# Two more slots for split weights, in which small operands lie in pairs, and a planner that knows turns at PSUM banks, 64-row operations and rows of loads

## The chip, the cores and the metric

The kernel runs on one core of one Trainium2 chip. The core has TensorE (PE in the profile, with PEld for its weight loads), VectorE (DVE), ScalarE (ACT), GpSimd (POOL) and SyncE (SP), which issues most of the loads. The metric is the device time of one execution, in microseconds (us); smaller is better.

## The reference

A decoder trunk of two layers, for 256 tokens of width 1024 and 256 memory tokens. Layer 0 mixes tokens by a gated MLP (12 groups of 64, chunks of 128), layer 1 by causal attention (12 heads of 64). Beside either mixer runs a cross-attention of 4 heads into the memory tokens. After each mixer and each feed-forward stands a LayerNorm with a scaled residual.

```python
def swiglu(x, w_in, w_out):
    g, u = jnp.split(x @ w_in, 2, axis=-1)
    return (jax.nn.silu(g) * u) @ w_out

def reference(x, mem, ...):
    for i in range(DEPTH):                       # 2
        if i % 2 == 0:
            h = x @ a_w_in[li]
            u, v, q_mem = jnp.split(h, [W_MIX, 2 * W_MIX], axis=-1)
            mix = gmlp_mixer(u, v, ...)          # gelu(u) * (W_s layer_norm(gelu(v)) + b), W_s causal
        else:
            h = x @ b_w_in[li]
            q, k, v, q_mem = jnp.split(h, ...)
            mix = moba_attention(q, k, v)        # 256 tokens are one block: causal attention
        mem_out = memory_cross_attention(q_mem, mem, w_mem_kv[i])
        sub = jnp.concatenate([mix, mem_out], axis=-1) @ w_mix_out[i]
        x = layer_norm(ALPHA * x + sub, ln_mix_g[i], ln_mix_b[i])
        x = layer_norm(ALPHA * x + swiglu(x, w_ffn_in[i], w_ffn_out[i]), ln_ffn_g[i], ln_ffn_b[i])
    return x
```

All is float32. D_FF is 2816, eleven chunks of 256 columns.

## The kernel before

**Products.** A float32 operand is split into two halves in the fp32r form: `hi`, a cast (ACT), and `lo = x - hi` (DVE). A product is three passes, hi·hi, hi·lo and lo·hi (`PASSES`). In the feed-forward, the first product of most pairs of chunks goes by Strassen and Winograd's seven products `M1` to `M7` in place of eight. They need sums of weight blocks and of x blocks (`Aa`, `Ac`, `SfM`, `SgM`), and their results are put together from PSUM (`Xf`, `Yf`, `Zf` for layer 0, with g for layer 1) into `m1`, `m5` and so on. `sgf` is the silu of a gate, `m5f` the gated chunk before it is transposed (`tpf`), and `htf` the transposed chunk, split in two halves for the second product (`fof`).

**Weights.** Weights come in units of 1 MB (128 x 2048 float32) into six buffers `raw_*`. Each unit is two halves, and each half takes one slot `spl_*` (128 x 2 x 1024): the ACT CAST writes its hi, then the DVE TENSOR_TENSOR its lo. `HALF_BUFS` is the number of these slots. A raw buffer is free for the next load when the lo of its last half is done; some units are then made from others, by a DVE addition in place or by an accumulating load that POOL issues. Loads are issued by SP (hard queue in the code) and POOL (soft queue), in the order of need.

**Small operands.** `ht` (transposed chunks), `memT` (transposed memory tokens) and `qks` (the queries of a pair of heads) are [128, 2, 512] each and have four buffers of their own, tag `hm`.

**Attention.** `stack_k` and `stack_q` move 64-row halves of a projection: `kkm` (hi, ACT casts of 64 rows) and `klm` (lo, DVE on 64 rows) for the memory keys, `qks` and `klq` for layer 1. Scores `s`, exponentials `pb` with row sums `zb`, transposes `pt` to `pT`, then `pv` and the mixed tile `mix1_n`, which is split too: an ACT cast, then a DVE subtraction. The output projection takes `spl_o1_*` halves (`opc`). It is followed by the LayerNorm and by the transposes of its result into `x3T` (x1T in layer 0), and there the feed-forward of the layer begins.

**What sets the order.** No instruction stands in the order of the program's text. `Plan` records all operations, `deadlines()` gives each a due time counted back from TensorE's order, and `simulate()` runs the recorded operations through a cost model (`Op.cost`, and class `Wire` for loads), choosing at each step the operation that can start first and is due first. It does so five times, with other settings (`TRIALS`), and the order with the least idle TensorE is issued by `emit()`. TensorE's own order is that of the text. Operations added by `either` (copies and scalings) may go to ACT or DVE, whichever the plan gives them to. On the chip each engine runs its list strictly in order, each instruction waiting on semaphores for what it reads or overwrites. So every recorded instruction has the line of `emit`, L574, and is told apart by its tiles.

Of the kernel before, what the change touches and what calls it, by code (L numbers as in the profile page):

```python
# [34 lines left out]
RAW_BUFS = 6  # L35
HALF_BUFS = 10
NFF = D_FF // 256
# [150 lines left out]
class Buffer(View):  # L188

    def __init__(self, pool, space, tag, bufs, shape, dtype, name):  # L190
# [9 lines left out]
        self.psum, self.whole = pool == "ps", False  # L200
        self.tile, self.log, self.slot, self.left, self.last = None, [], None, 0, 0.0


class Op:
    def __init__(self, n, engine, name, args, kw):
# [5 lines left out]
        self.before, self.after, self.opens = {}, [], []  # L211
        self.late, self.other = None, None
        self.cost()

# [30 lines left out]
class Wire:  # L245

    HARD, SOFT, BOTH, LANES = ((7000, 250), (30000, 370), (1e12, 428)), 223, (155, 123), 8
    SPARE = 1200, 1800

# [6 lines left out]
    def issue(self, op, t):  # L256
        self.run(t, [self.hard, self.soft])
        if op.engine == "sync":
            self.sent.append(op)
        (self.soft if op.engine == "gpsimd" else self.hard).append([op, t + 2350, op.bytes])  # L260
        self.run(1e12, [[list(x) for x in q] for q in (self.hard, self.soft)])

    def run(self, until, queues):
        hard, soft = queues
        now = self.now
        while (hard or soft) and now < until:
# [5 lines left out]
            for q, r, a in zip(queues, rates, live):  # L272
                if a:
                    q[0][2] -= (stop - now) * r
                    if q[0][2] < 1:
                        op = q.pop(0)[0]
                        op.end = stop + 100
                        op.sure = stop + (self.SPARE[op.engine == "gpsimd"] if stop > 20000 else 200)
            now = stop
# [4 lines left out]
class Plan:  # L284
# [90 lines left out]
    def order(self):  # L375
        self.deadlines()
        best = None
        for trial in self.TRIALS:
            for op in self.ops:
                for b in op.roots:  # L380
                    b.slot, b.last, b.left, b.moves = None, 0.0, 0, []
            for op in self.ops:
# [11 lines left out]
    def simulate(self, slip, idle, margin):  # L394
        lost, table, whole = 0, None, set()
        by_late = {e: sorted((op for op in self.ops if op.engine == e), key=lambda op: (op.late, op.n)) for e in ("vector", "scalar")}
# [27 lines left out]

        def opening(op):

            t0 = max([at[op.n]] + [o.sure for o in op.moves])
            if op.engine == "sync":
# [35 lines left out]
        while len(out) < len(self.ops):  # L464
            best, again = None, False
            for e in self.ENGINES:
# [4 lines left out]
                else:  # L471
                    cands = ready[e]
                c = [(max(free[e], t), op) for op in cands for t in (opening(op),) if t is not None]
                if not c:
# [39 lines left out]
            if e == "scalar" and op.name == "activation" and op.args[2] not in (AF.Identity, table):  # L514
                table = op.args[2]
                t += 1283
            if e == "tensor" and t > free[e] + 1:
                t += 95
# [38 lines left out]
            for b in op.roots:  # L557
                b.left -= 1
                b.last = max(b.last, end + 35)
                if op.name == "dma_start":  # L560
                    b.moves.append(op)
# [106 lines left out]
def build(chip, tc, ins, out):  # L668
    ET = mybir.EngineType
    with (  # L670
# [322 lines left out]
        class Ffn:  # L993
# [10 lines left out]
            def ht_tile(self, c):  # L1004
                if c not in self.hts:
                    self.hts[c] = tile_of("act", [P, 2, 512], F32R, "hm", f"ht{self.nm}{c}", 4).rearrange(
                        "p s (k t) -> p s k t", k=2)
                return self.hts[c]
# [250 lines left out]
        for j in range(4):  # L1259
            t = tile_of("act", [P, 2, 512], F32R, "hm", f"memT{j}", 4)  # L1260
            split(t[:, 0, :], t[:, 1, :], mraws[j])
# [83 lines left out]
        def qk_half(hp, j):  # L1345
# [3 lines left out]
            if j == 0:  # L1349
                st = tile_of("act", [P, 2, 512], F32R, "hm", f"qks{hp}", 4).rearrange("p a (b t) -> p a b t", b=2)  # L1350
                qks[hp] = st, klq[:, hp % 2]
                stack_q(lambda par: st[:, 0, par, :], t)
# [162 lines left out]
```

## Time and profile before

| what | value |
|---|---|
| runs, us | 564.18, 563.02, 563.37; median 563.37 |
| profiled execution, us | 563.18, its span 561.5 |
| granted TensorE clock, mean | 0.997 |
| PE busy | 548.5 us (98%), 3028 matmuls |
| DVE busy | 503.4 us (90%), 673 instructions |
| ACT busy | 370.0 us (66%), 563 instructions |
| POOL busy | 33.7 us (6%) |
| DMA | 132.52 MB, mean 236 GB/s |

The program runs through layer 0's mixer (to about 96 us), its feed-forward (to about 265), layer 1's projections and attention (to about 372), its feed-forward (to about 554), and 7 us after the last matmul. Rows of the timeline and of the groups name what is written and what is read (`out<-in`) without buffer numbers. In square brackets stands how long the engine was idle before the row and what ended the idle time. A row of several like instructions gives their number (x12). The ends of matmuls are modelled, so where two stretches of TensorE are compared, it is by their starts.

### The profile page before, as it was taken

Reading aid. Unit: us, or ns where it says so; the run is one execution under the profiler, and the core shown is the slowest. Engines: PE = TensorE matmul, PEld = TensorE weight load, DVE = VectorE, ACT = ScalarE, POOL = GpSimd, SP = SyncE. Lnnn points to the kernel's source line nnn. Section 1 sums busy time; section 2 is a strip of 40 time slices with the busy share of each in tenths; the row PEclk is TensorE's granted clock in tenths of the full one; section 3 lists DMA queues with packets and bytes.
Section 4 is the critical chain, followed back from the end, with each engine's and each line's share of the span. In section 5 each row is a group of like instructions: output and inputs, shape, how many; then the busy total and the mean of one; then the engine's idle time right before and its main releaser. Section 6 shows DMA issues by size and latency. Waiting matters only on the chain.

```text
span 561.5 us, 8058 instructions
## 1 busy us (share of the span) xinstructions
PE 548.5 (98%) x3028; PEld 473.2 (84%) x3028; DVE 503.4 (90%) x673; ACT 370.0 (66%) x563; POOL 33.7 (6%) x45
## 2 busy tenths in 40 slices
PE   8999999999999999999999999999999999999995
PEld 7999979878887888887899989788778888888884
DVE  5789979999999989989987898679999999999975
ACT  6876745596649486666466988557857495957620
POOL 2011000000000010000000000100000000100001
PEclk9999999999999999999999999999999999999998
DMA  8999753567897969889557253834488989797902
GB/s 288 400 384 350 306 210 116 149 151 274 204 395 183 375 187 336 253 248 355 222 222 295 84 189 138 163 113 151 86 302 210 392 200 392 176 353 212 296 5 76
DMA packets 23496, 132.52 MB, mean 236 GB/s; under 512 B 2592, under 2 KB 6304, under 8 KB 9376
## 3 DMA queue, kind: packets, MB, share of 16 engines
q1 hardware_dynamic: 20000, 109.45, 50.0%
q0 software_dynamic: 3024, 22.02, 21.1%
q10 hardware_dynamic: 432, 0.52, 0.3%
q8 instruction: 24, 0.39, 0.3%
q14 instruction: 16, 0.13, 0.1%
HBM read 120.46 MB, written 1.05 MB: 216 GB/s over the span
## 4 chain that ended last, share of the span: by engine, by line
PE 61%; DVE 18%; DMA 9%; ACT 6%; issue 4%; SPq 0%; DVEq 0%; ACTq 0%; POOLq 0%
PE fog L574 10%; PE Xg L574 7%; DVE spl_s_M L574 6%; DMA raw_s<-in_w 4%; PE opa L574 4%; PE Zg L574 4%; PE qk L574 4%; PE fof L574 3%; PE pu L574 3%; PE bv L574 3%; PE Xf L574 3%; DMA raw_s<-raw_s 3%; DVE raw_s L574 3%; PE opc L574 2%; PE va L574 2%
## 5 line engine op out<-in xcount | busy, mean ns | idle before, releaser
L574 DVE TENSOR_TENSOR spl_s_M<-raw_s,spl_s_M 128x1024 fp32r<-128x1024 f32 x140 | 164.9, 1225 | 3.2 <-ACT spl_s_M L574 3.0
L574 ACT CAST spl_s_M<-raw_s 128x1024 fp32r<-128x1024 f32 x140 | 139.7, 1051 | 37.9 <-DVE raw_s L574 15.3
L574 ACT CAST spl_w<-raw_w 128x1024 fp32r<-128x1024 f32 x44 | 45.7, 1054 | 29.3 <-DMA raw_w<-in_w 26.2
L574 PE MATMUL fof<-spl_w,htf 128*128 128x512 f32 x264 | 63.9, 392 | 0.0
L574 PE MATMUL fog<-spl_w,htg 128*128 128x512 f32 (+1 forms) x282 | 63.9, 378 | 0.0
L574 PEld LDWEIGHTS fog<-spl_w,htg 128*128 128x128 f32 x282 | 50.1, 188 | 9.4
L574 PEld LDWEIGHTS fof<-spl_w,htf 128*128 128x128 f32 x264 | 49.0, 188 | 9.9
L574 DVE TENSOR_TENSOR spl_w<-raw_w,spl_w 128x1024 fp32r<-128x1024 f32 x44 | 53.7, 1225 | 1.5 <-ACT spl_w L574 1.5
L574 DVE TENSOR_TENSOR raw_s<-raw_s,raw_s 128x2048 f32<-128x2048 f32 x19 | 43.5, 2292 | 0.0
L574 PE MATMUL qk<-x2T,spl_qk 128*128 128x256 f32 x288 | 36.4, 284 | 0.8 <-DVE mix L574 0.8
L574 PEld LDWEIGHTS qk<-x2T,spl_qk 128*128 128x128 f32 x288 | 35.2, 191 | 1.0 <-DVE mix L574 1.0
L574 PE MATMUL Xg<-spl_s_M,SgM 128*128 128x512 f32 x120 | 29.2, 391 | 0.7 <-DVE SgM L574 0.7
L574 PE MATMUL Zf<-spl_s_M,SfM 128*128 128x512 f32 x120 | 29.2, 392 | 0.3 <-DVE htf L574 0.3
L574 PE MATMUL Zg<-spl_s_M,SgM 128*128 128x512 f32 x120 | 28.8, 389 | 0.0
L574 PE MATMUL Xf<-spl_s_M,SfM 128*128 128x512 f32 x120 | 28.8, 389 | 0.0
L574 PE MATMUL Xf<-spl_s_M,x1T 128*128 128x512 f32 x120 | 28.3, 390 | 0.0
L574 PE MATMUL Xg<-spl_s_M,x3T 128*128 128x512 f32 x120 | 28.2, 389 | 0.0
L574 PEld LDWEIGHTS Xg<-spl_s_M,SgM 128*128 128x128 f32 x120 | 22.4, 188 | 5.7 <-DVE SgM L574 1.2
L574 PEld LDWEIGHTS Zf<-spl_s_M,SfM 128*128 128x128 f32 x120 | 22.3, 188 | 5.6 <-DVE htf L574 1.0
L574 PEld LDWEIGHTS Xf<-spl_s_M,x1T 128*128 128x128 f32 x120 | 22.5, 188 | 4.8
L574 PEld LDWEIGHTS Xg<-spl_s_M,x3T 128*128 128x128 f32 x120 | 22.5, 188 | 4.7
L574 PEld LDWEIGHTS Zg<-spl_s_M,SgM 128*128 128x128 f32 x120 | 22.5, 188 | 4.7
(246 smaller groups left out, 1005.0 us busy)
## 6 DMA issues: line engine op xcount, KB each, us to landing
raw_s<-in_w SPq DMA_DIRECT2D x40, 1024.0 KB, 7.4
raw_w<-in_w SPq DMA_DIRECT2D x22, 1024.0 KB, 9.1
raw_s<-in_w POOLq DMA_DIRECT2D x11, 1024.0 KB, 9.0
raw_s<-raw_s POOLq DMA_DIRECT2D x10, 1024.0 KB, 7.8
raw_o<-in_w SPq DMA_DIRECT2D x8, 1024.0 KB, 6.8
raw_qk<-in_w SPq DMA_DIRECT2D x6, 1024.0 KB, 5.1
raw_u<-in_w SPq DMA_DIRECT2D x3, 1024.0 KB, 12.0
raw_bv<-in_w SPq DMA_DIRECT2D x4, 768.0 KB, 8.2
```

The source lines that it names most:

```text
L574: getattr(getattr(self.nc, c.engine), c.name)(*map(real, c.args), **{k: real(v) for k, v in c.kw.items()})
```

## The change

- `HALF_BUFS` goes from 10 to 12, and the four buffers of tag `hm` are gone. Their memory is the same: 12 slots of 8 KB a partition, against 10 and four of 4 KB. `ht` of chunks c and c+1 (chunk 0 alone), `memT` 0 and 1, 2 and 3, and `qks` of an even and the next odd pair of heads lie together in one `spl` slot, which is free again when both are done.
- A PSUM buffer remembers when each engine last used it (`used`), and in the plan an operation on another engine waits for that end plus 35 ns (`turn`).
- In the plan an ACT or DVE operation that works on other rows than the one before it on its engine starts only when that one is done, plus 25 ns (`Op.rows`).
- In the plan of loads the margins `SPARE` go from 1200 and 1800 ns to 600 and 800, and a load that comes in a row behind another, or a soft load that shared the wire, is put 2000 ns later (`SKEW`).

```diff
-HALF_BUFS = 10
+HALF_BUFS = 12
...
+        ap = (self.writes or self.reads)[0].ap
+        self.rows = ap.offset // ap.ap[0][0], ap.ap[0][1]
...
-    SPARE = 1200, 1800
+    SPARE, SKEW = (600, 800), 2000
...
+                    if all(live):
+                        soft[0][3] = True
                     if q[0][2] < 1:
-                        op = q.pop(0)[0]
-                        op.end = stop + 100
-                        op.sure = stop + (self.SPARE[op.engine == "gpsimd"] if stop > 20000 else 200)
+                        op, _, _, burst = q.pop(0)
+                        if q:
+                            q[0][3] = q[0][1] <= stop
+                        op.end = stop + 100 + (self.SKEW if burst and stop > 20000 else 0)
+                        op.sure = op.end + (self.SPARE[op.engine == "gpsimd"] if stop > 20000 else 100)
...
+        def turn(op, e):
+
+            return max([0.0] + [t + 35 for b in op.roots if b.psum for e2, t in b.used.items() if e2 != e])
+
+        def opening(op, e):
+
+            t0 = max([at[op.n], turn(op, e)] + [o.sure for o in op.moves])
...
+            if e in by_late:
+                was, done = rows.get(e, (op.rows, 0.0))
+                if was != op.rows:
+                    t = max(t, done + 25)
+                rows[e] = op.rows, t + op.call.lat
...
+                b.used[e] = end
...
-                    self.hts[c] = tile_of("act", [P, 2, 512], F32R, "hm", f"ht{self.nm}{c}", 4).rearrange(
-                        "p s (k t) -> p s k t", k=2)
+                    mates = [c, c + 1] if c else [c]
+                    t = tile_of("spl", [P, 2, 1024], F32R, "spl", f"ht{self.nm}{c}", HALF_BUFS)
+                    for j, m in enumerate(mates):
+                        self.hts[m] = t[:, j, :].rearrange("p (s k t) -> p s k t", s=2, k=2)
...
-            t = tile_of("act", [P, 2, 512], F32R, "hm", f"memT{j}", 4)
+            if j % 2 == 0:
+                both = tile_of("spl", [P, 2, 1024], F32R, "spl", f"memT{j}", HALF_BUFS)
+            t = both[:, j % 2, :].rearrange("p (s n) -> p s n", s=2)
...
-                st = tile_of("act", [P, 2, 512], F32R, "hm", f"qks{hp}", 4).rearrange("p a (b t) -> p a b t", b=2)
-                qks[hp] = st, klq[:, hp % 2]
+                if hp % 2 == 0:
+                    both = tile_of("spl", [P, 2, 1024], F32R, "spl", f"qks{hp}", HALF_BUFS)
+                    for n in range(2):
+                        qks[hp + n] = both[:, n, :].rearrange("p (a b t) -> p a b t", a=2, b=2), klq[:, n]
+                st = qks[hp][0]
```

What the plan makes of it: TensorE's order stays. The rest moves a little everywhere: DVE has 667 operations where it had 675 and ACT 536 where it had 528, since 20 copies and scalings go from DVE to ACT and 12 the other way. Recorded instructions now have line L590. Three places follow.

The first is DVE where layer 0's feed-forward begins (`klm`: the memory keys' lo; `spl_s0_1_M1_*`: lo of the weights of M1; `Aa10`: a block of x; `x1T`: lo of the feed-forward's input). Before:

```order
L574 SCALAR_TENSOR_TENSOR xres_771<-xres_771,rsa1_1129,gb0mix_650 128x512 x2
L574 TENSOR_TENSOR klm_116<-hkm1_1085,kkm10_1161 64x256 x2
L574 TENSOR_TENSOR klm_116<-hkm1_1085,kkm11_1170 64x256 x2
L574 TENSOR_TENSOR spl_s0_1_M1_0_1068<-raw_s0_1_11_882,spl_s0_1_M1_0_1068 128x1024
L574 COPY Aa10_1214<-pta10_1201 128x512
L574 TENSOR_TENSOR x1T_1092<-pta10_1201,x1T_1092 128x4x128
```

The same place of the changed kernel:

```order
L590 SCALAR_TENSOR_TENSOR xres_746<-xres_746,rsa1_1127,gb0mix_650 128x512 x2
L590 TENSOR_TENSOR spl_s0_1_M1_0_1066<-raw_s0_1_11_887,spl_s0_1_M1_0_1066 128x1024
L590 TENSOR_TENSOR spl_s0_1_M1_1_1078<-raw_s0_1_11_887,spl_s0_1_M1_1_1078 128x1024
L590 TENSOR_TENSOR klm_116<-hkm1_1083,kkm10_1159 64x256 x2
L590 TENSOR_TENSOR klm_116<-hkm1_1083,kkm11_1169 64x256 x2
L590 TENSOR_TENSOR x1T_1090<-pta10_1196,x1T_1090 128x4x128
```

Both halves of M1's lo now stand ahead of the four `klm` operations, and the copy `Aa10` has gone to ACT.

The second is ACT at the first pair of chunks of layer 0's feed-forward (`sgf3`: the gate of chunk 3; `spl_w0_3_0`: hi of weights of the second product; `spl_s0_5_*`: hi of the next pair's weights). Before:

```order
L574 CAST spl_w0_3_0_1724<-raw_w0_3_1664 128x1024
L574 CAST spl_s0_5_M2_0_1739<-raw_s0_5_21_1678 128x1024
L574 ACTIVATE sgf3_1747<-Xf3_1508 128x512
L574 CAST spl_s0_5_M5_0_1753<-raw_s0_5_11_1638 128x1024
L574 CAST spl_s0_5_M5_1_1760<-raw_s0_5_11_1638 128x1024
```

And the same place of the changed kernel:

```order
L590 CAST spl_w0_3_0_1730<-raw_w0_3_1661 128x1024
L590 CAST spl_s0_5_M5_0_1742<-raw_s0_5_11_1635 128x1024
L590 ACTIVATE sgf3_1749<-Xf3_1504 128x512
L590 CAST spl_s0_5_M5_1_1753<-raw_s0_5_11_1635 128x1024
L590 CAST spl_s0_5_M2_0_1762<-raw_s0_5_21_1681 128x1024
```

The cast that reads `raw_s0_5_21`, the unit loaded last, now stands two rows behind `sgf3` and no longer ahead of it; a cast of an older unit has its place.

The third is DVE where layer 1's feed-forward begins (`x3T`: lo of its input; `Ac`: blocks of x; `spl_r1_0_B_1`: lo of the weights of chunk 0; `m1g1`: a product of chunk 1). Before:

```order
L574 TENSOR_TENSOR m1g1_3831<-m1g1_3831,Yg1_3839 128x512
L574 TENSOR_TENSOR spl_r1_0_B_1_3774<-raw_r1_0_B_3341,spl_r1_0_B_1_3774 128x1024
L574 COPY Ac10_3888<-ptc10_3874 128x512
L574 TENSOR_TENSOR x3T_3785<-ptc10_3874,x3T_3785 128x4x128
L574 TENSOR_TENSOR x3T_3785<-ptc11_3879,x3T_3785 128x4x128
L574 TENSOR_TENSOR spl_s1_1_M5_0_3804<-raw_s1_1_11_2941,spl_s1_1_M5_0_3804 128x1024
L574 TENSOR_TENSOR spl_s1_1_M5_1_3812<-raw_s1_1_11_2941,spl_s1_1_M5_1_3812 128x1024
```

And in the changed kernel:

```order
L590 TENSOR_TENSOR m1g1_3823<-m1g1_3823,Yg1_3833 128x512
L590 TENSOR_TENSOR spl_s1_1_M5_0_3829<-raw_s1_1_11_3049,spl_s1_1_M5_0_3829 128x1024
L590 COPY Ac10_3882<-ptc10_3870 128x512
L590 COPY Ac11_3887<-ptc11_3875 128x512
L590 TENSOR_TENSOR x3T_3775<-ptc10_3870,x3T_3775 128x4x128
L590 TENSOR_TENSOR x3T_3775<-ptc11_3875,x3T_3775 128x4x128
L590 TENSOR_TENSOR spl_s1_1_M5_1_3838<-raw_s1_1_11_3049,spl_s1_1_M5_1_3838 128x1024
```

The lo of `spl_r1_0_B_1` has gone up, ahead of the statistics of the second token tile's LayerNorm, and that of `spl_s1_1_M3_0` stands among them, `M5_0` has come ahead of the x3T operations, and the copy `Ac11` has come over from ACT.

More of the change, by code (lines that the diff above doesn't have):

```diff
@@ L200, in __init__ @@
         self.psum, self.whole = pool == "ps", False
-        self.tile, self.log, self.slot, self.left, self.last = None, [], None, 0, 0.0
+        self.tile, self.log, self.slot, self.left, self.last, self.used = None, [], None, 0, 0.0, {}
 class Op:
@@ L259, in issue @@
             self.sent.append(op)
-        (self.soft if op.engine == "gpsimd" else self.hard).append([op, t + 2350, op.bytes])
+        (self.soft if op.engine == "gpsimd" else self.hard).append([op, t + 2350, op.bytes, False])
         self.run(1e12, [[list(x) for x in q] for q in (self.hard, self.soft)])
@@ L380, in order @@
                 for b in op.roots:
-                    b.slot, b.last, b.left, b.moves = None, 0.0, 0, []
+                    b.slot, b.last, b.left, b.moves, b.used = None, 0.0, 0, [], {}
             for op in self.ops:
@@ L394, in simulate @@
     def simulate(self, slip, idle, margin):
-        lost, table, whole = 0, None, set()
+        lost, table, whole, rows = 0, None, set(), {}
         by_late = {e: sorted((op for op in self.ops if op.engine == e), key=lambda op: (op.late, op.n)) for e in ("vector", "scalar")}
@@ L423, in free_at @@
             return max([b.last] + [o.sure for o in b.moves]) if b else 0.0
-        def opening(op):
-            t0 = max([at[op.n]] + [o.sure for o in op.moves])
+        def turn(op, e):
+            return max([0.0] + [t + 35 for b in op.roots if b.psum for e2, t in b.used.items() if e2 != e])
+        def opening(op, e):
+            t0 = max([at[op.n], turn(op, e)] + [o.sure for o in op.moves])
             if op.engine == "sync":
@@ L472, in simulate @@
                     cands = ready[e]
-                c = [(max(free[e], t), op) for op in cands for t in (opening(op),) if t is not None]
+                c = [(max(free[e], t), op) for op in cands for t in (opening(op, e),) if t is not None]
                 if not c:
```

## The prediction, made before the changed kernel was run

> **What bounds the kernel now.** I read the busy times first, then windows of the stages, then TensorE's waits, and then the timelines of three engines at each wait.
>
> ```profile
> PE 548.5 (98%) x3028; PEld 473.2 (84%) x3028; DVE 503.4 (90%) x673; ACT 370.0 (66%) x563; POOL 33.7 (6%) x45
> ```
>
> ```profile
> 116.00:200.00 84.00, 83.49 (x374) 68.38 (x375) 82.02 (x80) 58.67 (x71) 4.92 (x6) 1.00 0.85 275
> 391.00:419.00 28.00, 26.28 (x116) 20.64 (x115) 28.00 (x32) 19.18 (x25) 1.52 (x2) 1.00 0.62 208
> ```
>
> The first fence is from the page: TensorE is busy for 548.5 of 561.5 us. The second gives, by window, the length, then the busy time of PE, PEld, DVE, ACT and POOL, the granted clock, the DMA share and GB/s. DVE works 82.02 of 84 us in one stretch of the first feed-forward, and all 28 us of the start of the second. So TensorE is the bound, and DVE comes close behind it: where DVE is late, TensorE waits. TensorE's order doesn't change and it does the same matmuls, so the change can win only the waits (engine, tile, what it waited for; total, times, longest):
>
> ```profile
> PE qk L574 <- DVE mix L574: 0.8, 1, 0.8
> PE Xg L574 <- DVE SgM L574: 0.7, 1, 0.7
> PE tpf L574 <- DVE hf L574: 0.7, 1, 0.7
> PE tpf L574 <- DVE m5f L574: 0.5, 2, 0.3
> PE tpg L574 <- DVE m1g L574: 0.5, 1, 0.5
> PE tpg L574 <- DVE m5g L574: 0.3, 1, 0.3
> PE tpg L574 <- DVE hg L574: 0.3, 1, 0.3
> PE Zf L574 <- DVE htf L574: 0.3, 1, 0.3
> ```
>
> A shown wait is less than what it costs, because the shown ends of matmuls are modelled. I measure the loss from start to start, with the pace of this row, 2.72 / 12 = 0.227 us for a matmul of 512 columns:
>
> ```profile
> 122.50 2.72 PE Xf L574 x12
> ```
>
> **The change, place by place.** *A, layer 0's feed-forward begins.* TensorE, then DVE (two of four like rows), then ACT (two of three):
>
> ```profile
> 112.53 2.88 PE L574 MATMUL Xf<-spl_s_M,x1T 128*128 128x512 f32 x12
> 116.13 0.88 PE L574 MATMUL tpf<-ident,hf 128*128 128x128 f32 x4 [0.71 <-DVE hf L574]
> ...
> 97.08 0.42 DVE L574 TENSOR_TENSOR klm<-hkm,kkm 64x256 fp32r<-64x256 f32 x1 [0.54 <-ACT kkm L574]
> ...
> 99.65 0.43 DVE L574 TENSOR_TENSOR klm<-hkm,kkm 64x256 fp32r<-64x256 f32 x1 [0.43 <-ACT kkm L574]
> ...
> 97.53 0.37 ACT L574 CAST kkm<-hkm 64x256 fp32r<-64x256 f32 x1 [0.48 <-DVE klm L574]
> ...
> 99.25 0.37 ACT L574 CAST kkm<-hkm 64x256 fp32r<-64x256 f32 x1 [0.48 <-DVE klm L574]
> ```
>
> From 112.53 to 116.13 are 3.60 us for 12 matmuls worth 2.72: 0.88 lost (0.17 more than the shown 0.71; I add 0.16 to the other shown waits). DVE and ACT take turns at `klm` and `kkm`: DVE is idle four times, 0.54 + 3 x 0.43 = 1.83 us. Between there and 116 DVE is full. In the changed order both lo of M1 (1.2 us each) stand ahead of the four `klm`, so ACT's casts have over 2 us to get done, and the copy `Aa10` (a 128x512 DVE operation, 0.69 in place B) goes to ACT. DVE's lead is about 1.83 + 0.6 = 2.4 us, and `hf` wants 0.88. Between 0 (the four still take turns) and 0.88 I take 0.85.
>
> By the Trainium skill (PSUM — Partial Sum Buffer, section on bank collisions), two engines may be at one bank at once if they are in different quadrants of partitions; a cast of the other 64 rows would then not have to wait for `klm`, and the turns would be no fixed cost. By that rule three of the four gaps, some 1.3 us, would have another cause and stay; the lead would be 1.1, and I would set the sum 0.3 lower. The rows here show the casts waiting 0.48 for DVE each time, and the row decides.
>
> *B, the gate of chunk 3, and the wait behind it.* TensorE, ACT, DVE:
>
> ```profile
> 169.70 0.27 PE L574 MATMUL tpf<-ident,m1f 128*128 128x128 f32 x1
> 170.10 0.33 PE L574 MATMUL tpf<-ident,m5f 128*128 128x128 f32 x1
> ...
> 170.84 3.01 PE L574 MATMUL fof<-spl_w,htf 128*128 128x512 f32 x12
> 174.10 1.66 PE L574 MATMUL Zf<-spl_s_M,SfM 128*128 128x512 f32 x6 [0.26 <-DVE htf L574]
> ...
> 165.29 1.06 ACT L574 CAST spl_w<-raw_w 128x1024 fp32r<-128x1024 f32 x1 [4.39 <-DMA raw_w<-in_w]
> 167.78 1.05 ACT L574 CAST spl_s_M<-raw_s 128x1024 fp32r<-128x1024 f32 x1 [1.43 <-DMA raw_s<-in_w]
> 168.73 0.59 ACT L574 ACTIVATE sgf<-Xf 128x512 f32<-128x512 f32 x1
> ...
> 169.35 0.69 DVE L574 SCALAR_TENSOR_TENSOR m5f<-m5f,sgf 128x512 f32<-128x512 f32 x1 [0.94 <-ACT sgf L574]
> 169.96 3.49 DVE L574 TENSOR_TENSOR spl_s_M<-raw_s,spl_s_M 128x1024 fp32r<-128x1024 f32 x3
> 173.37 0.69 DVE L574 TENSOR_TENSOR htf<-tpf,htf 128x512 fp32r<-128x512 f32 x1
> ```
>
> ACT stands at the cast of M2, whose load lands at 167.7, and the gate `sgf` behind it starts at 168.73. In the changed order a cast of a unit that is long there has this place, so `sgf` starts when TensorE's product is done, over 1 us sooner; and `htf`, which has three lo ahead of it here (3.49 us), has one lo and one copy (1.22 + 0.6). The loss is 0.29 at `m5f` (0.40 us between the two transposes; the seven from 170.10 to 170.84 take 0.74, so 0.11 would do) and 3.26 - 2.72 = 0.54 at `Zf`: 0.83. I take 0.7, between 0.3 (the gate alone) and 0.83.
>
> *C, the two shown waits of `m5f`* (0.5 together, with the ends 0.8), at later pairs: the first has the same cause, a gate behind four casts of a unit just landed, and three of these move behind it: 0.4 of 0.43. At the other nothing moves near the gate: 0.1 of 0.37. In all 0.5, between 0 and 0.8.
>
> *D, attention.* TensorE waits for `mix1_0`:
>
> ```profile
> 333.48 2.77 PE L574 MATMUL qk<-x2T,spl_qk 128*128 128x256 f32 x21 [0.76 <-DVE mix L574]
> ...
> 331.87 1.22 DVE L574 TENSOR_TENSOR spl_o<-raw_o,spl_o 128x1024 fp32r<-128x1024 f32 x1
> 333.00 0.42 DVE L574 TENSOR_TENSOR mix<-pv,mix 128x256 fp32r<-128x256 f32 x1
> ```
>
> The loss is 0.76 + 0.15. In the changed order `mix1_0` stands ahead of the scalings of `pb`, and the weight's lo (1.22) is gone from ahead of it: I take 0.7, between 0.3 and 0.91. Against it stands what now gets thin here: the same stage turns more 64-row work round, and the cover of the other scores is small.
>
> ```profile
> 324.33 0.88 DVE L574 TENSOR_TENSOR klq<-qk,qks 64x256 fp32r<-64x256 f32 x2 [0.32 <-ACT qks L574]
> ...
> 325.32 0.28 PE L574 MATMUL s<-klq,qks 128*128 128x128 f32 x1
> ```
>
> `klq` ends at 325.21 for a matmul at 325.32: 0.11 of cover. One lo put ahead of such a step costs up to 1.2. I put 0.7 for new waits, between 0 and 2.4 (two of them in full).
>
> *E, layer 1's feed-forward begins.* TensorE, then DVE:
>
> ```profile
> 400.22 0.71 PE L574 MATMUL Xg<-spl_s_M,SgM 128*128 128x512 f32 x2
> 401.66 1.65 PE L574 MATMUL Xg<-spl_s_M,SgM 128*128 128x512 f32 x6 [0.72 <-DVE SgM L574]
> ...
> 367.44 1.22 DVE L574 TENSOR_TENSOR spl_r_A<-raw_r_A,spl_r_A 128x1024 fp32r<-128x1024 f32 x1 [1.84 <-ACT spl_r_A L574]
> 389.44 0.69 DVE L574 TENSOR_TENSOR x3T<-ptc,x3T 128x512 fp32r<-128x512 f32 x1 [0.65 <-ACT x3T L574]
> 390.42 0.69 DVE L574 TENSOR_TENSOR x3T<-ptc,x3T 128x512 fp32r<-128x512 f32 x1 [0.29 <-ACT Ac L574]
> ```
>
> The losses: `SgM` 1.44 - 2 x 0.227 = 0.99; `hg`, `m1g`, `m5g` (0.3 + 0.5 + 0.3 shown) with the ends 1.5; together 2.5. From 391 to 419 DVE has no gap, so whatever it has done before 391 comes off these waits one for one. Two lo (`r1_0_B_1` and `M3_0`, 1.22 each) go up to where DVE is idle (1.84 in one row); `M5_0` fills the gaps of 0.65 and 0.29; against that the copy `Ac11` comes to DVE (0.6). The lead is 1.2 + 0.9 - 0.6 = 1.5 us until the place of `M3_0`, and 2.7 after it. For the moved lo ACT must cast sooner too, and it needs slots for it; the two more slots give them. The first two waits (1.4) go, and most of the others: I take 1.9, between 0.8 and 2.5.
>
> Edits that cost nothing: pairs in one slot have the same casts and lo as before, of the same sizes; the copies that go to ACT fall on an engine busy 66%; of the loads a few small rows swap places. The tail after 554 keeps its order.
>
> **The sum:** 0.85 + 0.7 + 0.5 + 0.7 + 1.9 - 0.7 = 3.95 us. The profiled execution took 563.18 (span 561.5), so 559.2 in its terms; the median of the runs is 563.37, 0.19 above it, so I predict 559.4. If every loss above went and no new wait came (0.88 + 0.83 + 0.8 + 0.91 + 2.5 = 5.9), it would be 557.5; with the lower ends (0 + 0.3 + 0 + 0.3 + 0.8 - 2.4 = -1.0), 564.4. Some tenths more lie in waits not costed here, so 557.0 is the lower end.
>
> **Rivals.** *The waits only move: no change.* DVE is the bound in all but name (28.00 of 28, 82.02 of 84), its summed work falls by under 2 us of 503, and an order that is early at one place is late at the next. For it: those windows. Against it: in places A and E DVE's gaps before the full stretch are themselves filled (1.83 and 0.94 us), which no later place takes back, since TensorE, not DVE, sets the pace from 419 on. It would give 562.9 to 563.9.
>
> *Half the leads carry.* The gaps at `klm` stay because the casts are in the same turns, and E gains only `SgM`: 0 + 0.7 + 0.3 + 0.4 + 1.0 - 0.7 = 1.7, so 561.7.
>
> *Slower: short slots in the attention make loads late.* `qks` now takes weight slots, and the lo of the `spl_o1` halves stand 8 to 13 us later in DVE's order; a raw buffer is free only after them, so the loads of `raw_r1_0_B` and `raw_s1_1_12`, and POOL's loads behind them, go out later.
>
> ```profile
> 356.56 0.88 POOL L574 DMA_DIRECT2D raw_s<-in_w  x1 [2.61 <-DVE mix L574]
> ...
> DMA to landing us min/median/max: 4.8/7.8/12.6
> ```
>
> The last of them goes out at 356.56 and takes up to 12.6, so lands at 369. I put it 6 us later, at 375, and its cast at about 379 in the changed order: 4 us are to spare. From there each us is one of TensorE's: a load 9 us later than I put it costs 5 us, eats all gains and gives 564.4. Against it: the median load here takes 7.8.
>
> *Planned too close.* The margins of loads fall to half, which would put casts of late units ahead of gates, as in B. The orders I compared show the reverse (the new 2 us push such casts back), so this is part of the half gain.
>
> **How the numbers follow.** What the measurement can tell from no change is about 0.2%, 1.1 us. My forecast (a gain of 2.5 us or more): 0.60. Half the gain (1.1 to 2.5): 0.18. No change: 0.13. Slower: 0.09. Faster is thus 0.78. The range goes from 557.0 to 563.2: it leaves out the slower case, half of no change, and a little at the low end, in all some 0.18. The forecast's own range is 557.0 to 560.9.
>
> **What would show it.** In the profile after, TensorE's waits for `hf`, `htf`, the first `m5f`, `mix` and `SgM` are gone or under 0.2; the four `klm` stand together with no gaps; `sgf` of chunk 3 starts about 1 us earlier against TensorE; DVE between 391 and 419 has gaps again. TensorE's busy time stays at 548. I am wrong if a new wait of over 0.5 stands in the attention (`s` or `qk` waiting for `klq`), if casts wait for DMA right ahead of a gate, or if the load that POOL issues lands after 379.

## The result, and the profile after

The changed kernel takes 557.62 us in the median of four runs (556.42 to 558.08), against 563.64 for the kernel before (563.02 to 564.18): a ratio of 0.989, with a 95% interval of 0.987 to 0.991, so 6.0 us less. Executions more than 1.5% above the fastest of their kernel are left out of all medians and ratios here. The profiled execution took 556.42, with a span of 554.7.

The page's busy times, TensorE's waits (all that are shown), and two windows of the changed kernel; the second window is the stretch that was 391 to 419 before:

```profile
PE 545.8 (98%) x3028; PEld 473.4 (85%) x3028; DVE 502.1 (91%) x665; ACT 371.0 (67%) x571; POOL 34.3 (6%) x45
```

```profile
PE warmup L744 <- DVE mhalf L741: 1.1, 1, 1.1
PE tpf L590 <- DVE m5f L590: 0.7, 2, 0.4
```

```profile
116.00:200.00 84.00, 84.00 (x385) 69.75 (x384) 81.28 (x78) 55.54 (x66) 4.34 (x5) 1.00 0.85 273
...
385.00:412.00 27.00, 27.00 (x122) 21.77 (x121) 26.77 (x31) 17.10 (x24) 1.59 (x2) 1.00 0.60 195
```

Of the eight rows of waits in the prediction one is left, `m5f`. DVE still does 81.28 of 84 us and 26.77 of 27, but TensorE now works all of both windows. TensorE's busy time is 545.8, where I had put 548: with the same 3028 matmuls, 2.7 us of what went had counted as busy. In place A (ACT, DVE, TensorE):

```profile
94.28 3.02 ACT L590 CAST kkm<-hkm 64x256 fp32r<-64x256 f32 x8 [2.78 <-PE hkm L590]
...
95.32 2.35 DVE L590 TENSOR_TENSOR spl_s_M<-raw_s,spl_s_M 128x1024 fp32r<-128x1024 f32 x2
97.59 1.72 DVE L590 TENSOR_TENSOR klm<-hkm,kkm 64x256 fp32r<-64x256 f32 x4
...
114.28 0.60 PE L590 MATMUL tpf<-ident,hf 128*128 128x128 f32 x4
```

The eight casts run in a row, the four `klm` too, without a gap, and `hf` is there in time. In B (ACT, DVE, TensorE) and in D (DVE, TensorE):

```profile
165.74 0.59 ACT L590 ACTIVATE sgf<-Xf 128x512 f32<-128x512 f32 x1
...
166.36 0.69 DVE L590 SCALAR_TENSOR_TENSOR m5f<-m5f,sgf 128x512 f32<-128x512 f32 x1 [0.53 <-ACT sgf L590]
...
168.16 2.98 PE L590 MATMUL fof<-spl_w,htf 128*128 128x512 f32 x12
170.98 1.75 PE L590 MATMUL Zf<-spl_s_M,SfM 128*128 128x512 f32 x7
...
328.01 0.41 DVE L590 TENSOR_TENSOR mix<-pv,mix 128x256 fp32r<-128x256 f32 x1
...
329.65 0.28 PE L590 MATMUL sm<-klm,qqm 128*128 128x256 f32 x1
329.77 1.48 PE L590 MATMUL qk<-x2T,spl_qk 128*128 128x256 f32 x11
```

`Zf` starts 2.82 us after `fof` (3.26 before), and `qk` 0.12 after the last `sm` (0.76 of shown wait before). In E, DVE:

```profile
374.62 1.22 DVE L590 TENSOR_TENSOR spl_r_B<-raw_r_B,spl_r_B 128x1024 fp32r<-128x1024 f32 x1
...
382.25 1.22 DVE L590 TENSOR_TENSOR spl_s_M<-raw_s,spl_s_M 128x1024 fp32r<-128x1024 f32 x1
383.38 1.28 DVE L590 COPY Ac<-ptc 128x512 f32<-128x512 f32 x2
384.73 1.29 DVE L590 TENSOR_TENSOR x3T<-ptc,x3T 128x512 fp32r<-128x512 f32 x2
```

The lo of `r1_0_B_1` and `M5_0` stand where they were to stand, and the gaps of 0.65 and 0.29 ahead of `x3T` are gone.

TensorE's order is the same in every kernel here, so time can be put down to stretches between the same two matmuls. The table gives, for the profile of each run, how much longer a stretch is than in the kernel before, in us, from the starts of the matmuls that bound it. Start: to the 61st matmul. A: to the `Zf` that stands at 142.93 before. B: to 175.83. C: to 265.93. Attention: to 362.62. E: to 419.49. End: the rest. Behind them stand the median of the timed runs and the ratio to the kernel before on the same chip.

| kernel | start | A | B | C | attention | E | end | all but start | median, ratio |
|---|---|---|---|---|---|---|---|---|---|
| before, length | 10.75 | 131.13 | 32.90 | 90.10 | 96.69 | 56.87 | 134.70 | | 563.64 |
| changed | -0.95 | -1.35 | -0.96 | +0.48 | -1.93 | -2.35 | +0.29 | -5.82 | 557.62, 0.989 |
| changed, again | -0.22 | -1.36 | -0.95 | +0.80 | -1.93 | -2.30 | +0.34 | -5.41 | 557.29, 0.9877 |
| slots only | +0.14 | -0.01 | +0.27 | +0.69 | +2.24 | -2.20 | +0.28 | +1.27 | 564.74, 1.0021 |
| slots and load rule | +1.14 | +0.73 | -0.46 | +0.48 | +2.26 | -2.20 | +0.41 | +1.20 | 563.77, 1.001 |
| planner only | +0.19 | -1.37 | -0.95 | -0.97 | -1.90 | +0.11 | -0.09 | -5.17 | 558.39, 0.9912 |
| without load rule | -0.73 | -1.37 | -0.40 | +0.71 | -1.92 | -2.29 | +0.22 | -5.05 | 557.84, 0.9901 |
| without turns | +0.26 | -0.75 | -0.64 | +0.95 | +0.20 | -1.65 | +0.34 | -1.55 | 562.18, 0.9977 |
| without 64-row rule | -0.14 | -1.37 | -0.95 | +0.93 | +0.21 | -2.29 | +0.49 | -3.00 | 560.17, 0.9933 |
| eleven slots | +0.80 | -1.37 | -0.95 | -0.97 | -1.90 | -1.68 | -0.06 | -6.93 | 556.55, 0.9866 |
| m5 moved | -0.57 | -1.36 | -0.95 | -0.39 | -1.90 | -2.35 | -0.06 | -7.01 | 557.41, 0.9883 |
| m5 moved, again | -0.63 | -1.36 | -0.96 | -0.16 | -1.90 | -2.34 | +0.17 | -6.55 | 556.79, 0.9869 |
| before, lo ahead of klm | +0.49 | -0.48 | +0.12 | +0.78 | 0.00 | 0.00 | +0.02 | +0.44 | 563.2, 0.9987 |
| before, casts first | 0.00 | -0.13 | -0.07 | +0.65 | 0.00 | 0.00 | -0.03 | +0.42 | 563.91, 1.0 |

Two things in it are chance. The start has the same order in all kernels, and its length differs by up to 2.1 us from run to run, since TensorE waits there for the first weights (0.3 to 1.6 us in the rows of waits, or none). The 0.73 that "slots and load rule" has in A is of that kind too: the five matmuls behind the 61st lose all of it. And in C the last two kernels have the order of the kernel before, yet lose 0.65 and 0.78 us against its profile: C as a whole is known to some 0.8 us only. Otherwise A, B, attention and E repeat to about 0.1.

### The profile page after: what moved, and what is told of

Same layout as the page of the kernel before. It is cut to its first block, busy times and chain, and to the rows that moved or that the text cites. A ratio compares the mean times of both kernels' runs of the same rounds, so it can differ in the third digit from the quotient of the medians.

```text
span 554.7 us, 7993 instructions
## 1 busy us (share of the span) xinstructions
PE 545.8 (98%) x3028; PEld 473.4 (85%) x3028; DVE 502.1 (91%) x665; ACT 371.0 (67%) x571; POOL 34.3 (6%) x45
## 4 chain that ended last, share of the span: by engine, by line
PE 72%; DVE 14%; DMA 7%; issue 4%; ACT 2%; SPq 0%; DVEq 0%; ACTq 0%; POOLq 0%
PE fog L590 11%; PE Xg L590 10%; DVE spl_s_M L590 7%; PE qk L590 6%; PE Zg L590 5%; DMA raw_s<-in_w 4%; PE opc L590 4%; PE opa L590 4%; PE pu L590 3%; PE bv L590 3%; PE pvm L590 3%; PE Yg L590 2%; PE va L590 2%; PE hkm L590 2%; PE hqm L590 2%
## 5 line engine op out<-in xcount | busy, mean ns | idle before, releaser
L590 DVE TENSOR_TENSOR spl_s_M<-raw_s,spl_s_M 128x1024 fp32r<-128x1024 f32 x140 | 164.7, 1221 | 6.3 <-ACT spl_s_M L590 6.1
L590 ACT CAST spl_s_M<-raw_s 128x1024 fp32r<-128x1024 f32 x140 | 139.6, 1050 | 38.1 <-DMA raw_s<-in_w 23.4
L590 PE MATMUL fof<-spl_w,htf 128*128 128x512 f32 x264 | 63.9, 392 | 0.0
L590 PE MATMUL fog<-spl_w,htg 128*128 128x512 f32 (+1 forms) x282 | 63.9, 378 | 0.0
L590 ACT CAST spl_w<-raw_w 128x1024 fp32r<-128x1024 f32 x44 | 45.6, 1051 | 23.4 <-DMA raw_w<-in_w 20.9
L590 PEld LDWEIGHTS fog<-spl_w,htg 128*128 128x128 f32 x282 | 50.2, 188 | 9.4
L590 PEld LDWEIGHTS fof<-spl_w,htf 128*128 128x128 f32 x264 | 49.0, 188 | 9.9
L590 DVE TENSOR_TENSOR spl_w<-raw_w,spl_w 128x1024 fp32r<-128x1024 f32 x44 | 53.7, 1221 | 2.9 <-ACT spl_w L590 2.9
L590 DVE TENSOR_TENSOR raw_s<-raw_s,raw_s 128x2048 f32<-128x2048 f32 x19 | 43.5, 2288 | 0.1
L590 PE MATMUL qk<-x2T,spl_qk 128*128 128x256 f32 x288 | 36.3, 283 | 0.0
L590 PEld LDWEIGHTS qk<-x2T,spl_qk 128*128 128x128 f32 x288 | 35.2, 192 | 0.0
L590 PE MATMUL Zg<-spl_s_M,SgM 128*128 128x512 f32 x120 | 29.1, 390 | 0.0
L590 PE MATMUL Xg<-spl_s_M,SgM 128*128 128x512 f32 x120 | 29.0, 390 | 0.0
L590 PE MATMUL Zf<-spl_s_M,SfM 128*128 128x512 f32 x120 | 29.0, 390 | 0.0
L590 PE MATMUL Xf<-spl_s_M,SfM 128*128 128x512 f32 x120 | 28.8, 389 | 0.0
L590 PE MATMUL Xf<-spl_s_M,x1T 128*128 128x512 f32 x120 | 28.3, 390 | 0.0
L590 PE MATMUL Xg<-spl_s_M,x3T 128*128 128x512 f32 x120 | 28.3, 390 | 0.1
L590 PEld LDWEIGHTS Xf<-spl_s_M,x1T 128*128 128x128 f32 x120 | 22.4, 188 | 5.2 <-issue 0.6
L590 PEld LDWEIGHTS Xg<-spl_s_M,x3T 128*128 128x128 f32 x120 | 22.5, 188 | 5.1 <-issue 0.4
L590 PEld LDWEIGHTS Zg<-spl_s_M,SgM 128*128 128x128 f32 x120 | 22.5, 188 | 5.0 <-DVE SgM L590 0.4
L590 PEld LDWEIGHTS Xf<-spl_s_M,SfM 128*128 128x128 f32 x120 | 22.5, 188 | 4.7
L590 PEld LDWEIGHTS Xg<-spl_s_M,SgM 128*128 128x128 f32 x120 | 22.4, 188 | 4.8 <-DVE SgM L590 0.2
```

The lines of the kernel that those rows point to most:

```text
L590: getattr(getattr(self.nc, c.engine), c.name)(*map(real, c.args), **{k: real(v) for k, v in c.kw.items()})
```

## The experiments

**One: slots alone.** The changed kernel with the planner of before.

```diff
-    SPARE, SKEW = (600, 800), 2000
+    SPARE, SKEW = (1200, 1800), 0
...
-                        op.sure = op.end + (self.SPARE[op.engine == "gpsimd"] if stop > 20000 else 100)
+                        op.sure = stop + (self.SPARE[op.engine == "gpsimd"] if stop > 20000 else 200)
...
-            return max([0.0] + [t + 35 for b in op.roots if b.psum for e2, t in b.used.items() if e2 != e])
+            return 0.0
...
-                if was != op.rows:
+                if False:
```

> Twelve slots and pairs, with the planner of before (no turns, no 64-row rule, old load margins). By its order klm and kkm still take turns, the cast of M2 still stands ahead of sgf3; mix1_0 stands behind one lo and one scaling; r1_0_B_1 and M5_0 stand ahead of the second LayerNorm of layer 1. Theory (each place follows its own order rows): waits for hf (0.9 us) and for htf and m5f at chunk 3 (0.8) stay, mix falls from 0.9 to under 0.4, layer 1's feed-forward start loses 0.5 to 1.2 in place of 2.5; together about 561.5 us. Rival (the memory is what counts: slots let ACT cast early everywhere): near the changed kernel, 558 us, with hf and htf gone too. Rival (waits only move): 563 us.

Measured: 564.74 us, ratio 1.0021 (1.0008 to 1.0034): slower than before by 0.2%. TensorE's longest waits of this kernel:

```profile
PE tpf L590 <- DVE m5f L590: 1.5, 3, 0.8
PE pt L590 <- DVE mix L590: 1.4, 2, 1.0
PE qk L590 <- DVE mix L590: 1.2, 1, 1.2
PE warmup L744 <- DVE mhalf L741: 1.1, 1, 1.1
PE va L590 <- ACT spl_v L590: 0.9, 1, 0.9
PE tpf L590 <- DVE hf L590: 0.7, 1, 0.7
```

The theory held for A and B, gave E too little (2.20 for 1.3 to 2.0, nearly all that E gets in the end), and failed for the attention: `mix` was to fall under 0.4 and rose to 1.2, with 1.4 more at the transposes behind it. The gain of E is lost again there.

**Two: slots and the load rule.** As before, but with `SPARE, SKEW = (600, 800), 2000`.

> Slots and pairs and the plan's later loads (SPARE, SKEW), without turns and without the 64-row rule. By its order the gates of chunks 3 and 7 stand ahead of the casts of late units, klm and kkm still take turns. Theory: waits at chunk 3 (0.8) are gone, hf (0.9) stays, the rest as with slots alone: about 560.7 us. Rival (the load rule puts casts too late and PE waits for weights): over 562 us with PE waiting for spl tiles.

Measured: 563.77 us, 1.001 (1.0 to 1.0021), with the waits of the attention as in the first run. Against slots only, the load rule makes B 0.73 shorter, for 0.8 expected, and nothing else that can be told from chance. The wait for `htf` is gone, but `m5f` at chunk 3 still waits 0.22 us, though its gate stands ahead of the late cast here. The total fails for the same reason as in the first run.

**Three: the planner alone.** The three rules with ten slots and the four buffers of tag `hm`.

```diff
-HALF_BUFS = 12
+HALF_BUFS = 10
...
+                    self.hts[c] = tile_of("act", [P, 2, 512], F32R, "hm", f"ht{self.nm}{c}", 4).rearrange(
+                        "p s (k t) -> p s k t", k=2)
...
```

> The three planner rules with the ten slots and the four small buffers of before. By its order klm stand behind both lo of M1, sgf3 ahead of the late cast, mix1_0 behind one lo; r1_0_B_1 and M3_0 stay late at layer 1's feed-forward. Theory: hf, htf, mix go (about 2.7 us), layer 1's feed-forward start still loses 2 to 2.5: about 560.8 us. Rival (memory is what counts): 563 us. Rival (all from the planner): 558 us.

Measured: 558.39 us, 0.9912 (0.9896 to 0.9929). Its waits have all of E and nothing of A, B and the attention:

```profile
PE Xg L590 <- DVE SgM L590: 0.7, 1, 0.7
PE tpg L590 <- DVE m1g L590: 0.4, 1, 0.4
PE tpg L590 <- DVE hg L590: 0.3, 1, 0.3
PE tpg L590 <- DVE m5g L590: 0.3, 1, 0.3
```

The places came as expected, but for the attention (-1.90 in place of about -1) and C (-0.97). So the total lies 2.4 under the forecast of 560.8 and near the 558 of the last rival, which gave all to the planner; that rival falls all the same, as E gains nothing here (+0.11).

**Four: without the load rule.**

```diff
-    SPARE, SKEW = (600, 800), 2000
+    SPARE, SKEW = (1200, 1800), 0
...
-                        op.sure = op.end + (self.SPARE[op.engine == "gpsimd"] if stop > 20000 else 100)
+                        op.sure = stop + (self.SPARE[op.engine == "gpsimd"] if stop > 20000 else 200)
```

> The changed kernel with the old margins and no skew of loads. By its order only the gates of chunks 3 and 7 fall back behind the casts of late units, and M3_0 stays late at layer 1's feed-forward. Theory: chunk 3 loses 0.8 again, the feed-forward start of layer 1 some 1 us; about 559.3 us. Rival (margins of loads decide nothing, as loads land where they land): 557.6 us, like the changed kernel.

Measured: 557.84 us, 0.9901 (0.9886 to 0.9916), not to be told from the changed kernel, as the rival had it. B is 0.56 longer, less than 0.8, and that is the wait for `htf` alone: `m5f` at chunk 3 does not wait, though the late cast stands ahead of its gate again. E is as short as with M3_0's lo up front (-2.29), so M3_0 is not what made E.

**Five and six: without turns, and without the 64-row rule.** One line each of the first experiment's diff.

> The changed kernel without the rule on turns at PSUM buffers. By its order the four klm stand ahead of the lo of M1 again (their four gaps of 0.45 us come back), though the copy Aa10 stays on ACT; mix1_0 still stands ahead of the scalings. Theory (the rule on turns made place A, the rule on 64 rows made the attention): hf waits again 0.2 to 0.5 us, the attention is as in the changed kernel, and M3_0 late at layer 1's feed-forward costs nothing, as without the load rule: 557.9 to 558.3 us. Rival (turns made the attention too): mix and pt wait 1 us and more each, 560.5 us.

> The changed kernel without the rule on operations on other rows. By its order place A is as changed, but mix1_0 stands behind a weight's lo and two scalings and mix1_2 behind four scalings and a lo, as with slots alone. Theory: hf does not wait, while mix1_0, mix1_2 and the transposes behind them cost about 2.2 us more than in the kernel before and 4 more than in the changed one: 561.5 us. Rival (the rule on rows only shifts times by 25 ns and decides nothing): 557.6 us.

Measured: 562.18 us, 0.9977 (0.9964 to 0.9989), and 560.17, 0.9933 (0.9915 to 0.9951). I had given the attention to the 64-row rule alone. It is +2.24 with neither rule, +0.20 and +0.21 with one, -1.93 with both: each is worth some 2.1 us, and both theories fall in that point. Nor is place A the rule on turns alone: without it the turns of `kkm` and `klm` are back, and A is still 0.75 shorter than before, with the copy `Aa10` on ACT. What the rule on turns does in the attention is seen without it (ACT, DVE, TensorE):

```profile
352.53 0.74 ACT L590 CAST qks<-qk 64x256 fp32r<-64x256 f32 x2 [0.33 <-DVE klq L590]
353.77 0.37 ACT L590 CAST qks<-qk 64x256 fp32r<-64x256 f32 x1 [0.49 <-DVE klq L590]
354.16 0.37 ACT L590 CAST mix<-pv 128x256 fp32r<-128x256 f32 x1
...
354.56 0.42 DVE L590 TENSOR_TENSOR mix<-pv,mix 128x256 fp32r<-128x256 f32 x1 [0.83 <-ACT mix L590]
...
355.04 0.55 PE L590 MATMUL pt<-ident,pb 128*128 128x128 f32 x3 [1.31 <-DVE mix L590]
```

Without the rule the plan lets the casts of `qks` run beside `klq`, which reads the same PSUM buffer; on the chip they take turns, the cast of `mix` stands behind them on ACT, and TensorE waits 1.31. Without the 64-row rule the loss stands elsewhere than I had put it: 0.67 of the wait for `mix1_0` goes, and it is the transposes behind it that wait, until DVE is past its row `zm`.

```profile
335.50 0.52 PE L590 MATMUL pt<-ident,pb 128*128 128x128 f32 x3 [0.77 <-DVE zm L590]
```

**Seven and twelve: two products moved.** In the changed kernel's list the gated product `m5f7` goes ahead of the lo of `spl_s0_9_M2_0`, and that of `m5f9` ahead of the lo of `spl_bv1_0`; no other operation changes its place.

```diff
+    MOVES = (("vector", ("spl_s0_9_M2_0",), ("m5f7", "sgf7")), ("vector", ("spl_bv1_0",), ("m5f9", "sgf9")))
...
-        for op in self.order():
+        for op in self.moved(self.order()):
```

> The changed kernel with two operations moved by hand in DVE's order: the gated product of m5f7 goes ahead of the lo of M2 (it stood behind it), that of m5f9 ahead of the lo of spl_bv1_0. Nothing else moves. Theory (the two waits left, 0.46 and 0.52 us from start to start, are only DVE's order): both are gone and nothing takes their place, 556.7 us. Rival (the gate on ACT holds them): both stay, 557.6 us. Rival (the two lo that go back 0.6 us are then waited for by TensorE): 557.6 us with waits for spl tiles.

> The changed kernel with the two gated products moved by hand, beside the changed kernel on the same chip. Theory: 0.6 to 0.9 us less than the changed kernel in the median, since its profile showed the two stretches 0.57 and 0.31 us shorter and nothing longer. Rival (the start, where a wait for the first weights runs from 0 to 1.6 us from run to run, hides it): medians within 0.4 us.

Measured: 557.41 us, 0.9883 (0.9863 to 0.9902), and on another chip 556.79, 0.9869 (0.9854 to 0.9884), beside the changed kernel's 557.29 there. The two waits are gone and a small one ahead of `Xf` is left, here from experiment twelve:

```profile
PE va L613 <- ACT spl_v L613: 0.3, 1, 0.3
PE Xf L613 <- DVE m5f L613: 0.3, 1, 0.3
```

By place C is 0.9 us shorter than in the changed kernel both times. That is near the 0.8 of chance, but the two steps that were moved repeat better: from the matmul ahead of it to the first transpose of `m5f` are 0.11 and 0.23 us at chunks 7 and 9 in both runs, and 0.57 and 0.75, then 0.55 and 0.72, in the two runs of the changed kernel. The medians differ by 0.5 at most, less than the 0.6 to 0.9 expected, with intervals that overlap, so the gain is shown by the place and not by the time.

**Eight: both lo of M1 ahead of klm, in the kernel before.** Only DVE's list changes.

```diff
+    MOVES = (("vector", ("klm", "kkm10"), ("spl_s0_1_M1_0",)), ("vector", ("klm", "kkm10"), ("spl_s0_1_M1_1",)))
```

> The kernel before with one move by hand in DVE's order: both lo of M1 go ahead of the four klm. Buffers, copies and all else are as before. Theory (the gaps come from DVE and ACT taking turns at one PSUM buffer, and vanish when ACT has a lead): the four gaps of together 1.83 us fall to under 0.3, hf waits no more, place A from product start to start is 0.9 to 1.1 shorter: 562.6 us. Rival (the gaps are a fixed cost of 64-row operations): they stay, hf still waits 0.7, 563.5 us. Rival by the skill's rule on quadrants (the casts were never held up by klm): they stay as well.

Measured: 563.2 us, 0.9987 (0.9977 to 0.9998). A is 0.48 shorter, not 0.9 to 1.1, and the turns stay (ACT, then DVE):

```profile
95.66 1.88 ACT L597 CAST kkm<-hkm 64x256 fp32r<-64x256 f32 x5 [3.38 <-PE hkm L597]
99.67 0.37 ACT L597 CAST kkm<-hkm 64x256 fp32r<-64x256 f32 x1 [2.13 <-DVE klm L597]
...
99.22 0.41 DVE L597 TENSOR_TENSOR klm<-hkm,kkm 64x256 fp32r<-64x256 f32 x1
100.07 0.43 DVE L597 TENSOR_TENSOR klm<-hkm,kkm 64x256 fp32r<-64x256 f32 x1 [0.44 <-ACT kkm L597]
```

ACT has time for eight casts while DVE does the two lo, and stops after five: the sixth waits 2.13 us for the first `klm`. Only the first gap is gone, and `hf` comes 0.47 us sooner against TensorE. TensorE doesn't wait for it any more, partly because it is late itself: `x1T` stands behind the turns and both lo now, and `pf`, which reads it, loses 0.40. So my theory of the lead falls, and the first rival, a fixed cost of 64-row operations, isn't ruled out by this run.

**Nine: casts first, in the kernel before.** The list of each engine stays as it is; the last casts are only issued ahead of the first `klm` in the order common to all engines.

```diff
+        casts = [op for op in out[at:] if op.call.engine == "scalar" and op.writes and name(op.writes[0]) in ("kkm10", "kkm11")]
...
+        rest = [op for op in out[at:] if op not in casts]
+        return out[:at] + casts + rest
```

> The kernel before, in which the last kkm casts are issued ahead of the first klm in the order that is common to all engines. The list of each engine by itself is as before, word for word; only who waits for whom at the PSUM buffer that both read changes. Theory (the turns come from the common order: a cast that is issued behind a klm waits for it): the eight casts run in a row, the gaps of klm fall from 1.83 us to under 0.6 in all, hf waits no more or under 0.2, place A is 0.8 to 1.1 us shorter. Rival (the gaps are a cost of 64-row operations, or the klm wait for the casts anyway): the four gaps stay, place A as before.

Measured: 563.91 us, 1.0 (0.999 to 1.0009). The turns are gone, so they are no cost of 64-row operations:

```profile
95.17 3.01 ACT L584 CAST kkm<-hkm 64x256 fp32r<-64x256 f32 x8 [3.38 <-PE hkm L584]
...
98.22 1.73 DVE L584 TENSOR_TENSOR klm<-hkm,kkm 64x256 fp32r<-64x256 f32 x4 [1.67 <-ACT kkm L584]
```

But the first `klm` now waits for the last cast (95.17 + 3.01 = 98.18), 1.67 in one piece in place of 1.83 in four, and A wins only 0.13. Here who waits for whom at the PSUM buffer is decided by the common order, and the program's semaphores hold the buffer as a whole. Neither move alone gives the full gain: casts first leaves the 1.67 idle, and the two lo that would fill it leave the turns. They give 0.13 and 0.48, and the changed kernel, with both and the copy on ACT, 1.35. Both without the copy were not run; the 0.75 of experiment five, with the copy and neither move, says that the copy may have a good part in it.

**Ten: eleven slots.**

```diff
-HALF_BUFS = 12
+HALF_BUFS = 11
```

> The changed kernel with eleven slots. By its order the attention stays as in the changed kernel; at layer 1's feed-forward start r1_0_B_1 stands behind the second LayerNorm's statistics and M3_0 is late, M5_0 still stands ahead of x3T. Theory (what slots give there is the lo that stand ahead of the full stretch of DVE, 1.2 us each): between ten slots (24.4 us for this stretch) and twelve (22.0), so 22.6 to 23.6, and about 558.6 us. Rival (any slot more than ten is enough): 22.0 us and 557.6. Rival (twelve are needed): 24.4 us and 560.

Measured: 556.55 us, 0.9866 (0.9851 to 0.9881), on the chip where the changed kernel took 557.29, 0.9877 (0.9863 to 0.9892). E is 22.63 in the stretch for which I gave 22.6 to 23.6, and C is 1.45 to 1.77 shorter than in the changed kernel, more than the 0.8 of chance, which I had not expected and by which the total, 558.6, is missed. The wait of `m5f` at chunk 9 is gone, and at chunk 7 the product has no lo ahead of it.

```profile
225.88 2.28 DVE L590 TENSOR_TENSOR raw_s<-raw_s,raw_s 128x2048 f32<-128x2048 f32 x1
228.88 0.69 DVE L590 SCALAR_TENSOR_TENSOR m5f<-m5f,sgf 128x512 f32<-128x512 f32 x1 [0.71 <-ACT sgf L590]
```

Its median is the lowest of all, 0.7 under the changed kernel's on the same chip, though the intervals overlap. The twelfth slot thus wins 0.6 in E and, by the order that comes with it, loses more in C.

**Eleven: the changed kernel again.**

> The changed kernel once more, beside the next one on the same chip: 557.6 us; the waits of m5f at chunks 7 and 9 are there again, 0.46 and 0.52 us from start to start.

Measured: 557.29 us, as expected; the waits of `m5f` are 0.6 together.

## Why the prediction was right or wrong, point by point

The forecast was 559.4, the gain 4.0 for a measured 6.0. It held as a direction and in its range; of its terms those of A, B and E were right in sign and low by 0.3 to 0.5 each, that of C came to nothing, and the largest miss is the attention. That the 0.5 of C and the 0.7 of new waits, both absent, nearly cancel in the sum is luck.

- *A: 0.85, measured 1.35.* The place and the sign are right. The step that failed is the reason: "ACT's casts have over 2 us to get done". By experiment eight they don't use it. In the changed kernel the gaps go because all eight casts stand first in the common order too, which the list of one engine doesn't show. DVE then has `hf` 2.8 us sooner against TensorE, for the 2.4 that I had put. How much of the 1.35 is the turns and how much the copy stays open, as experiment five has 0.75 with the turns. The size was low because I counted the wait for `hf` alone: the second transpose behind it had 0.22 to give, and a later `Zf`, at 142.36 before, 0.20.
- *The turns and the rows.* In experiment nine the first `klm`, on 64 rows, starts 0.04 us after the last cast ends, though the casts of its rows were among the earlier ones: the program's semaphores keep the whole buffer apart. The Trainium skill (PSUM — Partial Sum Buffer, section "PSUM bank collisions raise a hardware error") says that engines in different quadrants of a bank may go together; whether the chip would allow that here, no run shows. The sum 0.3 lower, which I gave for that case, would have been further from the 1.35.
- *B: 0.7, measured 0.96.* The part of `htf` came by the mechanism named: without the load rule 0.56 is lost, all of it there. The part of the gate did not. I had put `sgf` over 1 us sooner, behind the cast of a unit that is long there, and it is 0.67 sooner against the start of its product (3.81 us after it, 4.48 before), because that cast waits for a DVE addition:

```profile
164.78 1.06 ACT L590 CAST spl_s_M<-raw_s 128x1024 fp32r<-128x1024 f32 x1 [1.29 <-DVE raw_s L590]
```

  The wait for `m5f` is gone without the load rule too, if A has its gain (experiment four), and stays with the rule and without the gain of A (experiment two, 0.22). So it seems to go by DVE's lead from A; no run moves that lead alone.
- *C: a gain of 0.5, measured none* (+0.48 and +0.80, where the kernel before's order lost 0.65 and 0.78 in other runs). The gate of chunk 7 did come sooner, but I had followed ACT's list and not DVE's. Before (ACT, DVE), and changed (ACT, DVE, TensorE):

```profile
231.43 0.60 ACT L574 ACTIVATE sgf<-Xf 128x512 f32<-128x512 f32 x1
...
232.06 0.69 DVE L574 SCALAR_TENSOR_TENSOR m5f<-m5f,sgf 128x512 f32<-128x512 f32 x1 [1.05 <-ACT sgf L574]
```

```profile
226.62 0.59 ACT L590 ACTIVATE sgf<-Xf 128x512 f32<-128x512 f32 x1
...
225.57 2.29 DVE L590 TENSOR_TENSOR raw_s<-raw_s,raw_s 128x2048 f32<-128x2048 f32 x1
227.78 1.22 DVE L590 TENSOR_TENSOR spl_s_M<-raw_s,spl_s_M 128x1024 fp32r<-128x1024 f32 x1
228.91 0.69 DVE L590 SCALAR_TENSOR_TENSOR m5f<-m5f,sgf 128x512 f32<-128x512 f32 x1
...
229.65 0.33 PE L590 MATMUL tpf<-ident,m5f 128*128 128x128 f32 x1 [0.30 <-DVE m5f L590]
```

  The gate is done at 227.21, and the product starts at 228.91, behind an addition and a lo. What else stands ahead of the consumer is what I had asked at other places and not here. The profile of before was at the good end of chance, too: from the transpose ahead to that of `m5f` it has 0.54 us, and experiments eight and nine, with the same order at this place, 1.06 and 0.76, where the changed kernel has 0.57 and 0.55. So the sooner gate may be worth 0.2 to 0.5 in other runs.
- *D and the new waits: 0.7 - 0.7 = 0, measured 1.93.* `mix1_0` gave 1.0. The new waits didn't come, and 0.84 went at later transposes, for which the prediction has only "some tenths more lie in waits not costed here". The slots alone do lose there (+2.24, near the 2.4 at the upper end of that term), but by waits for `mix` and not, as I had it, for `klq`; the rules on turns and on 64 rows take 2.1 each from it. So the step that failed is the 0.7 put against the gain: I had costed what the order moves and not what the two rules do in the stage where ACT and DVE share PSUM buffers. That they work by making the plan's times truer there is argued, from the turns in experiment five.
- *E: 1.9, measured 2.35*, nearly all of the 2.5 that were there. It is the slots' doing: +0.11 with ten, -1.68 with eleven, -2.2 to -2.35 with twelve in every order but that without turns (-1.65). Of my three causes, `M3_0` was not needed. The gaps that DVE was to have there again are 0.23 of 27 us.
- *What I hadn't foreseen:* 0.2 to 0.5 more at the end of layer 1 in most kernels with twelve slots. In the changed kernel 0.22 of it stands ahead of one `Xg`, at 505.89 before. Its cause is open.
- *The rivals.* Waits didn't just move: DVE is as full as before and TensorE waits less. The loads did go out later, those of `raw_r1_0_B` and `raw_s1_1_12` at 346.18 and 350.91 in place of 337.88 and 347.51, and POOL's last as here:

```profile
358.00 0.88 POOL L590 DMA_DIRECT2D raw_s<-in_w  x1 [0.31 <-issue]
```

  By the clock that is 1.4 us later. But TensorE is 4.7 us further on there, so against its work the load goes out 6.2 later, about the 6 that I had put. It lands some 12 us after its issue, at about 370 and not after 379, and no TensorE wait comes from it. A slower kernel was there to be had, with the slots alone, but by waits of `mix` and not by loads.

What is shown, by leaving each out: that E is the slots', that the attention needs both the rule on turns and that on 64 rows, that the wait for `htf` in B is the load rule's, and that neither move of A is enough alone. Not shown are how A divides between the turns and the copy, what takes away the gate's wait in B, why the end is longer, and that the lower median of eleven slots would hold over more runs.

## What to carry to other kernels

Where an engine's list is made by a planner, rules for what the engines share can be worth more than memory: here the slots alone cost 1.3 us besides the start, the rules alone won 5.2, and both together 5.4 to 5.8. When two engines read one PSUM buffer, look at the common order of issue and not only at each list, since here it decided who waits for whom. And at each wait follow both engines that feed it: taking away a late gate wins little while another operation stands ahead of its consumer.

## What the runs showed of the hardware that was not expected

- ACT casts and DVE subtractions that take turns at one PSUM buffer cost 0.85 us a pair (in experiment eight `klm` starts at 99.22 and 100.07), where four `klm` in a row take 1.72 us in the changed kernel, 0.43 each. Experiment nine shows that this is a matter of the order of issue.
- The wait for the first weights takes 1.0 us in one run of the changed kernel and does not show in another, with the same instructions in the same order; a difference of 1 us between two single profiles of this kernel can be that alone.
